# The last stage of a hybrid attention block on whole rows of 1024 columns, with the embedding vectors loaded earlier and the scalings behind the next tile's statistics

## The chip, the cores and the metric

The kernel runs on one core of a Trainium2 chip. Five kinds of engine work beside each other on it: TensorE (PE, its weight loads PEld) multiplies matrices into PSUM, VectorE (DVE) and ScalarE (ACT) work elementwise, GpSimd (POOL) does small work and issues the accumulating transfers, SyncE (SP) issues most of the others. The metric is the device time of one execution in microseconds; lower is better.

## The reference, cut to what matters

A block of a decoder: 16 meta tokens are put ahead of 512 rows of x, a layer norm with the embedding vectors `emb_ln_g` and `emb_ln_b` gives h, two attention branches run on one input projection, and their gated outputs are merged. The last stage adds the merged product to h, scaled by `DN_ALPHA`, normalizes each row of 1024 and applies `ln_g` and `ln_b`.

```python
h = layer_norm(concatenate([meta, x]), emb_ln_g, emb_ln_b)
for i in range(DEPTH):                              # DEPTH = 1
    proj = einsum('bld,dn->bln', h, w_in[i])        # ten parts of 1024 columns
    ...                                             # differential and stick-breaking attention: y_d, y_s
    br_d = einsum('blw,wd->bld', y_d * silu(g_d), w_br_diff[i])
    br_s = einsum('blw,wd->bld', y_s * silu(g_s), w_br_sb[i])
    merged = sigmoid(m_d + b_gate[i, 0]) * br_d + sigmoid(m_s + b_gate[i, 1]) * br_s
    y = einsum('bld,de->ble', merged, w_out[i])
    h = layer_norm(DN_ALPHA * h + y, ln_g[i], ln_b[i])
return h[:, N_META:]
```

## The kernel before, in words

All products are done in a fast fp32 form on split operands: a value a is a rounded high half and the remainder (a − high), and a product is three matmuls, high × high, high × low, low × high. The weights come as blocks of 128 × 512 (256 KB) through rings of buffers (`fetch`, line 144), ScalarE casts the high half (`hi`, line 183: `wh`), VectorE subtracts for the remainder (`lo`, line 188: `wl`). `wh` and `wl` are two tags with six buffers each; a block is split four blocks ahead of its use (`prep`).

The program has three parts. The start (norm of h, first queries) and everything behind the attention are fixed in the order in which they are written (`keep_order`). Between them lie 16 attention units (8 differential, 8 stick-breaking, interleaved with the projections of the next units); there a planner, which keeps its own timeline of engines and waits, sets the order on each engine. The later 11 units get keys and values by a seven-product scheme (line 690), and the two branch outputs too (`pair`, line 1065: pairs "BD" and then "BS", four each, with p from 0 to 3).

The last stage multiplies the merged rows (`MH`, `ML`) with the output weight in halves of 512 columns, `wo0` and `wo1`, each with its high and low half (`split_out`, lines 1126 and 1127, eight blocks of k per half). The loop runs over the two column halves c and, inside, over four row tiles t of 128 rows. A tile and half are 24 matmuls (line 1190) into one of three PSUM buffers; the last tile of the second half is done in two pieces of 256 columns. VectorE then adds the product to the scaled residual (line 1198) and takes statistics (line 1201). The residual, h again from x, is two VectorE instructions (lines 1161 and 1162) on 512 columns, done in the list `MEANWHILE` behind the tile's matmuls. Rows of x (`hr`) and the vectors (`eg`, `eb`) are loaded in halves of 512 by `load_half` into buffers of `wh` and `wl`; all eight `hr` halves and four vector halves are in place of twelve split weights.

When a tile has its second half, the statistics are aggregated (line 1206), GpSimd makes the reciprocal deviation `rs` in two small instructions (lines 296 and 297), and VectorE does, per 512 columns, a shift (line 1211: subtract the mean, times `ln_g`) and a scaling (line 1215: times `rs`, plus `ln_b`), in the order shift, scaling, shift, scaling, before it turns to the next tile. In the last tile ScalarE and GpSimd do the scaling of the last 256 columns (lines 1221 and 1222). SyncE writes the halves out (line 1227). `ln_g` and `ln_b` (`lgb`) are loaded by ScalarE's queue in the first tile, into buffers of the tag "two".

## Time and profile before

| | |
|---|---|
| time, median of 3 runs | 712.08 us (711.63 to 712.46) |
| profiled execution | 712.22 us, its span 710.4 us |
| busy: TensorE, VectorE, ScalarE, GpSimd | 697.5, 571.8, 439.2, 125.6 us |
| mean granted TensorE clock | 0.995 |
| last stage on TensorE | from 656.4 to 700.7 us |

The times on the right of a profile row are microseconds; in a timeline the first number is the start from the beginning of the span, the second the duration, and in brackets stands how long the engine was idle before and for what it waited. Matmuls overlap, so a busy TensorE is not yet one at its peak.

### The profile page before, as it was taken

To read this page: it belongs to the slowest core of one execution; us is meant where nothing else is said; L and a number is where in the kernel's file an instruction comes from. 1 tells how busy PE (TensorE), PEld (TensorE's weight loads), DVE (VectorE), ACT (ScalarE), POOL (GpSimd) and SP (SyncE) were. 2 spreads that over 40 slices of the span, in tenths; PEclk is the share of its full clock that TensorE was granted. 3 is DMA by queue.
4 is the path that set the end of the run, shared out by engine and by line. 5 is a ranking of instruction groups with operands and counts; after the bars stand their busy time and mean duration, and the time that the engine had idled before them with its cause. 6 is when DMAs were issued, how large, how long until landed. Compare 5 with 4: busy or idle time off the path is not lost.

```text
span 710.4 us, 13389 instructions
## 1 busy us (share of the span) xinstructions
PE 697.5 (98%) x4494; PEld 636.9 (90%) x4494; DVE 571.8 (80%) x1265; ACT 439.2 (62%) x1065; POOL 125.6 (18%) x143
## 2 busy tenths in 40 slices
PE   9999999999999999999999999999999999999994
PEld 8999999989999898988989998988889998999884
DVE  6888897878787777988878889976666788788897
ACT  5766676757667587776857777666455546455300
POOL 3214210212222111212123120000012102220002
PEclk9999999999999999999999999999999999999997
DMA  9368754879888876899897976646576748795902
GB/s 293 93 169 164 167 133 125 184 181 183 198 200 184 201 177 164 186 215 214 200 217 174 206 171 175 166 133 197 178 174 112 164 123 182 133 198 170 322 15 104
DMA packets 182182, 123.36 MB, mean 174 GB/s; under 512 B 9009, under 2 KB 165074, under 8 KB 182114
## 3 DMA queue, kind: packets, MB, share of 16 engines
q1 hardware_dynamic: 148130, 102.32, 50.1%
q0 software_dynamic: 33664, 19.14, 21.6%
q10 hardware_dynamic: 320, 1.06, 0.4%
q8 instruction: 35, 0.57, 0.3%
q14 instruction: 33, 0.27, 0.1%
HBM read 91.96 MB, written 9.44 MB: 143 GB/s over the span
## 4 chain that ended last, share of the span: by engine, by line
PE 86%; DVE 6%; DMA 3%; ACT 2%; issue 1%; POOL 1%; SPq 0%; ACTq 0%; DVEq 0%; POOLq 0%
PE q L690 16%; PE ps L496 12%; PE ps L494 12%; PE ps L495 12%; PE q L1065 10%; PE ps L510 7%; PE sc L754 6%; PE t L766 4%; DMA lgb<-in_ln_b_dram 1%; PE bank L385 1%; PE tv L723 1%; DVE hr L1215 1%; DMA xt<-in_x_dram 1%; PE av L922 1%; DMA raw<-in_w_out_dram 1%
## 5 line engine op out<-in xcount | busy, mean ns | idle before, releaser
L188 DVE TENSOR_TENSOR wl<-raw,wh 128x512 fp32r<-128x512 f32 x169 | 115.7, 691 | 43.7 <-ACT wh L183 42.2
L494 PE MATMUL ps<-hTh,wh 128*128 128x512 f32 x368 | 145.0, 394 | 0.0
L495 PE MATMUL ps<-hTl,wh 128*128 128x512 f32 x368 | 144.5, 393 | 0.0
L496 PE MATMUL ps<-hTh,wl 128*128 128x512 f32 x368 | 144.4, 392 | 0.0
L183 ACT CAST wh<-raw 128x512 fp32r<-128x512 f32 x169 | 104.4, 625 | 28.0 <-PE ps L495 15.3
L496 PEld LDWEIGHTS ps<-hTh,wl 128*128 128x128 f32 x368 | 69.2, 188 | 13.9
L495 PEld LDWEIGHTS ps<-hTl,wh 128*128 128x128 f32 x368 | 69.2, 188 | 13.1
L494 PEld LDWEIGHTS ps<-hTh,wh 128*128 128x128 f32 x368 | 69.2, 188 | 12.9
L146 POOL DMA_DIRECT2D rawk<-in_w_in_dram x44 | 60.8, 1642 | 96.9 <-DMA rawk<-in_w_in_dram 58.4
L754 PE MATMUL sc<-k,A 128*128 128x264 f32 (+3 forms) x320 | 65.9, 299 | 0.1
L1065 PE MATMUL q<-gh,wh 128*128 128x256 f32 x224 | 63.5, 283 | 0.2 <-ACT t L1074 0.2
L1065 PE MATMUL q<-gl,wh 128*128 128x256 f32 x224 | 63.4, 283 | 0.0
L1065 PE MATMUL q<-gh,wl 128*128 128x256 f32 x224 | 63.4, 283 | 0.0
L907 DVE TENSOR_TENSOR_SCAN e<-e,diag 128x528 f32<-128x528 f32 (+1 forms) x64 | 53.4, 848 | 7.5 <-ACT e L901 7.3
L754 PEld LDWEIGHTS sc<-k,A 128*128 128x128 f32 x320 | 50.3, 189 | 3.3 <-ACT e L901 0.3
L690 PE MATMUL q<-tS,wh 128*128 128x264 f32 x176 | 50.9, 290 | 0.9 <-DVE low L612 0.9
L690 PE MATMUL q<-tl,wh 128*128 128x264 f32 x176 | 50.2, 286 | 0.0
L690 PE MATMUL q<-tS,wl 128*128 128x264 f32 x176 | 50.2, 286 | 0.0
L510 PE MATMUL ps<-hTh,wh 128*128 128x264 f32 x160 | 46.4, 290 | 0.2 <-ACT k L632 0.2
L933 POOL DMA_DIRECT2D ys<-half x14 | 11.8, 840 | 195.9 <-ACT ys L932 119.2
L510 PE MATMUL ps<-hTh,wl 128*128 128x264 f32 x160 | 45.6, 286 | 0.0
L510 PE MATMUL ps<-hTl,wh 128*128 128x264 f32 x160 | 45.5, 285 | 0.0
(291 smaller groups left out, 1851.4 us busy)
## 6 DMA issues: line engine op xcount, KB each, us to landing
raw<-in_w_in_dram SPq DMA_DIRECT2D x141, 256.0 KB, 3.3
rawk<-in_w_in_dram POOLq DMA_DIRECT2D x44, 256.0 KB, 6.0
rawk<-in_w_in_dram SPq DMA_DIRECT2D x33, 256.0 KB, 3.9
k<-ks SPq DMA_DIRECT2D x60, 132.0 KB, 3.1
raw<-in_w_out_dram SPq DMA_DIRECT2D x16, 256.0 KB, 3.9
k<-ks SPq DMA_DIRECT2D x60, 66.0 KB, 2.8
A<-low SPq DMA_DIRECT2D x28, 128.0 KB, 2.8
raw<-in_w_br_diff_dram SPq DMA_DIRECT2D x12, 256.0 KB, 4.7
```

The costliest lines, as they stand in the source:

```text
L146: second[l] = [lambda raw=raw, x=x: g.dma_start(raw, x, accum_op=ALU.add) for x in more]
L183: s.copy(wh, raw)
L188: eng.tensor_tensor(wl, raw, wh.bitcast(F32), op=ALU.subtract)
L494: pe.matmul(ps, wh[:, k % 4, :], hTh[:, k, M:], start=(k == 0), stop=False)
L495: pe.matmul(ps, wh[:, k % 4, :], hTl[:, k, M:], start=False, stop=False)
L496: pe.matmul(ps, wl[:, k % 4, :], hTh[:, k, M:], start=False, stop=(k == KT - 1))
L510: pe.matmul(ps[:, :H2], a[:, k % 4, :], b[:, k, ts(c, H2)], start=(k == 0 and m == 0), stop=(k == KT - 1 and m == 2))
L690: pe.matmul(bank, a[:, k, :], b, start=start and k == 0 and j == 0, stop=k == 3 and j == 2, skip_group_check=not start)
L754: pe.matmul(ps[:, :n], q, K[:, m, k0:k0 + n], start=(m == 0), stop=(m == 1))
L766: pe.transpose(t[:, o:o + P], a[:, AOFF[i] + j * P:AOFF[i] + (j + 1) * P], ident)
L907: v.tensor_tensor_scan(rev, rev, diag[0][:, L - nk:][:, ::-1], 0.0, ALU.mult, ALU.max)
L1065: pe.matmul(bank, a[:, k, :], b[:, n, k, :], start=start and k == 0 and m == 0, stop=k == 3 and m == 2, skip_group_check=not start)
```

## The change

The split weights' halves share one tag `w2`: a buffer holds the high and the low half of a block. The rows of x, `hr`, become one buffer of 1024 columns per row tile, in the place of one split block, and so do `ln_g` and `ln_b`. The embedding vectors are whole too; they take buffers of the tag "two" and are loaded ahead of the second pair of the second branch (p = 1). The residual, the shift and the scaling are one instruction on 1024 columns each (the last tile scales in two halves). The scaling of a tile is held in `unfinished` until the next tile has its statistics; the third tile's follows its own shift at once. ScalarE and GpSimd have no part in the last tile's columns any more. The output is written by whole rows, the last tile by halves. `ln_g` and `ln_b` are loaded in the third tile of the first column half.

```diff
@@ -178,7 +178,8 @@
         item = items[h]
         assert not second.get(item)
         raw = raw0[:, h // 2, ts(h % 2, 4)] if item is None else sums.pop(h) if isinstance(item, tuple) else raws[item]
-        wh, wl = [wpool.tile([P, 4, P], F32R, tag=w, name=w, bufs=6) for w in ("wh", "wl")]
+        w2 = wpool.tile([P, 2, 4, P], F32R, tag="w2", name="w2", bufs=6)
+        wh, wl = w2[:, 0], w2[:, 1]
         split.append((raw, wh, wl))
         s.copy(wh, raw)
 
@@ -1133,8 +1134,13 @@
         state["ahead"] += 1
         prep(len(split))
 
+    vec = {}
     for p in range(4):
         steps = []
+        if p == 1:
+            for name, src in (("eg", emb_g), ("eb", emb_b)):
+                vec[name] = pair_of(name, n=512).rearrange("p a b -> p (a b)")
+                nc.sync.dma_start(vec[name], src.partition_broadcast(P))
         if p == 3:
             run([merge_gate(1, 7, MS[7])], [(4.4, further)])
             WO = [[hpool.tile([P, KT, 512], F32R, tag=f"hT{x}", name=f"wo0{x}") for x in "hl"]]
@@ -1142,46 +1148,39 @@
         run([pair("BS", p, G, MS[2 * p:2 * p + 2], lambda m, p=p: merged(2 * p + m))], steps)
 
 
-    def half(tag, name):
-        return wpool.tile([P, 4, P], F32, tag=tag, name=name, bufs=6).rearrange("p a b -> p (a b)")
-
-    vec, hrs = {}, [[None, None] for t in range(NB)]
-
-    def load_half(c):
-        tag = ("wh", "wl")[c]
-        for name, src in (("eg", emb_g), ("eb", emb_b)):
-            vec[name, c] = half({"eg": "wh", "eb": "wl"}[name], name)
-            nc.sync.dma_start(vec[name, c], src[ts(c, 512)].partition_broadcast(P))
-        for t in range(NB):
-            hrs[t][c] = half(tag, "hr")
-            nc.sync.dma_start(hrs[t][c], x[0, ts(t, P), ts(c, 512)])
-
-    def residual(t, c):
-        hr = hrs[t][c]
-        v.scalar_tensor_tensor(hr, hr, xmv[:, t, 0:1], vec["eg", c], op0=ALU.subtract, op1=ALU.mult)
-        v.scalar_tensor_tensor(hr, hr, xrs[:, t:t + 1], vec["eb", c], op0=ALU.mult, op1=ALU.add)
+    def whole(name):
+        return wpool.tile([P, 2, 4, P], F32, tag="w2", name=name, bufs=6).rearrange("p a b c -> p (a b c)")
+
+    hrs = []
+
+    def load_rows(t):
+        hrs.append(whole("hr"))
+        nc.sync.dma_start(hrs[t], x[0, ts(t, P), :])
+
+    def residual(t):
+        hr = hrs[t]
+        v.scalar_tensor_tensor(hr, hr, xmv[:, t, 0:1], vec["eg"], op0=ALU.subtract, op1=ALU.mult)
+        v.scalar_tensor_tensor(hr, hr, xrs[:, t:t + 1], vec["eb"], op0=ALU.mult, op1=ALU.add)
 
     for _, f in later:
         f()
     later.clear()
-    load_half(0)
     for k in range(5, KT):
         split_out(0, k)
-    load_half(1)
+        if k == 5:
+            load_rows(0)
     WO.append([lp.tile([P, KT, 512], F32R, tag=f"g{x}", name=f"wo1{x}") for x in "hl"])
-    lgb = [pair_of("lgb", n=512) for j in range(2)]
-    lgb = [t.rearrange("p a b -> p (a b)") for t in lgb]
+    lgb, unfinished = [], []
     sts = [lr.tile([P, 4, 6], F32, tag="fst", name="fst", bufs=4) for t in range(NB)]
-    MEANWHILE = [[lambda: residual(0, 0)] + [lambda k=k: split_out(1, k) for k in range(3)],
-                 [lambda: residual(1, 0)] + [lambda k=k: split_out(1, k) for k in range(3, 6)],
-                 [lambda: residual(2, 0)] + [lambda k=k: split_out(1, k) for k in range(6, 8)] + [lambda: residual(0, 1)],
-                 [lambda: residual(3, 0)] + [lambda t=t: residual(t, 1) for t in range(1, 3)],
-                 [lambda: residual(3, 1)], [], [], []]
+    MEANWHILE = [[lambda k=k: split_out(1, k) for k in range(3)] + [lambda: residual(0), lambda: load_rows(1)],
+                 [lambda k=k: split_out(1, k) for k in range(3, 6)] + [lambda: residual(1), lambda: load_rows(2)],
+                 [lambda k=k: split_out(1, k) for k in range(6, 8)] + [lambda: residual(2), lambda: load_rows(3)],
+                 [lambda: residual(3)], [], [], [], []]
     for c in range(2):
         for t in range(NB):
             st, final = sts[t], t == NB - 1
             for o, w in [(0, 256), (256, 256)] if final and c else [(0, 512)]:
-                r, hr = ds(o, w), hrs[t][c]
+                r, hr = ds(o, w), hrs[t][:, ts(c, 512)]
                 ps = pj.tile([P, 512], F32, tag="pj", name="pso")[:, :w]
                 products = [(k, m) for k in (0, 1, 2, 3, 4, 5, 7, 6) for m in ("hh", "hl", "lh")]
                 if t == 0 and c == 0:
@@ -1192,9 +1191,10 @@
                 if o == 0:
                     for work in MEANWHILE[NB * c + t]:
                         work()
-                    if t == 0 and c == 0:
-                        nc.scalar.dma_start(lgb[0][:, :], ln_g[0].partition_broadcast(P))
-                        nc.scalar.dma_start(lgb[1][:, :], ln_b[0].partition_broadcast(P))
+                    if t == 2 and c == 0:
+                        for src in (ln_g, ln_b):
+                            lgb.append(whole("lgb"))
+                            nc.scalar.dma_start(lgb[-1], src[0].partition_broadcast(P))
                 v.scalar_tensor_tensor(hr[:, r], hr[:, r], DN_ALPHA, ps, op0=ALU.mult, op1=ALU.add)
                 w = 256 if final else 512
                 for n in range(o // w, 2 if final and not c else o // w + 1):
@@ -1206,25 +1206,30 @@
             v.bn_aggr(mv, st[:, :4 if final else 2])
             rstd_of(lr, mv[:, 1:2], rs, P)
 
-            def shift(c, o, w):
-                a = hrs[t][c][:, ds(o, w)]
-                v.scalar_tensor_tensor(a, a, mv[:, 0:1], lgb[0][:, ds(512 * c + o, w)], op0=ALU.subtract, op1=ALU.mult)
-
-            def scale(c, o, w):
-                a = hrs[t][c][:, ds(o, w)]
-                v.scalar_tensor_tensor(a, a, rs, lgb[1][:, ds(512 * c + o, w)], op0=ALU.mult, op1=ALU.add)
-
-            shift(0, 0, 512)
-            if final:
-                a = hrs[t][1][:, 256:]
-                shift(1, 256, 256)
-                s.mul(a, a, rs)
-                g.tensor_tensor(a, a, lgb[1][:, 768:], op=ALU.add)
-            scale(0, 0, 512)
-            shift(1, 0, 256 if final else 512)
-            scale(1, 0, 256 if final else 512)
-            for h in range(2):
-                nc.sync.dma_start(out[0, ts(t, P), ts(h, 512)], hrs[t][h])
+            def shift(o, w, t=t, mv=mv):
+                a = hrs[t][:, ds(o, w)]
+                v.scalar_tensor_tensor(a, a, mv[:, 0:1], lgb[0][:, ds(o, w)], op0=ALU.subtract, op1=ALU.mult)
+
+            def scale(o, w, t=t, rs=rs):
+                a = hrs[t][:, ds(o, w)]
+                v.scalar_tensor_tensor(a, a, rs, lgb[1][:, ds(o, w)], op0=ALU.mult, op1=ALU.add)
+
+            def finish(scale=scale, t=t):
+                scale(0, D)
+                nc.sync.dma_start(out[0, ts(t, P), :], hrs[t])
+
+            if unfinished:
+                unfinished.pop()()
+            shift(0, D)
+            if not final:
+                unfinished.append(finish)
+                if t == NB - 2:
+                    unfinished.pop()()
+                continue
+            scale(0, 512)
+            nc.sync.dma_start(out[0, ts(t, P), :512], hrs[t][:, :512])
+            scale(512, 512)
+            nc.sync.dma_start(out[0, ts(t, P), 512:], hrs[t][:, 512:])
     keep_order(state["ends"], ORDERED[:1])
     keep_order(first, ORDERED + [mybir.EngineType.SP])
 
```

Three places show what this does to the order. First SyncE's queue, from the end of the second branch to the end of the program. Before (`raw` of `in_w_out` are blocks of the output weight):

```order
L144 DMA raw<-in_w_out_dram 128x512 x11
L1154 DMA eg<-in_emb_ln_g_dram 128x512
L1154 DMA eb<-in_emb_ln_b_dram 128x512
L1157 DMA hr<-in_x_dram 128x512 x4
L144 DMA raw<-in_w_out_dram 128x512 x3
L1154 DMA eg<-in_emb_ln_g_dram 128x512
L1154 DMA eb<-in_emb_ln_b_dram 128x512
L1157 DMA hr<-in_x_dram 128x512 x4
L144 DMA raw<-in_w_out_dram 128x512 x2
L1227 DMA out_dram<-hr 128x512 x8
```

With the change (`raw` and `rawa` of `in_w_br_sb` are the last pair's weights, lines are counted in the new file):

```order
L1143 DMA eg<-in_emb_ln_g_dram 128x1024
L1143 DMA eb<-in_emb_ln_b_dram 128x1024
L144 DMA raw<-in_w_in_dram 128x4x128
L144 DMA raw<-in_w_br_sb_dram 128x4x128
L144 DMA rawa<-in_w_br_sb_dram 128x4x128 x2
L144 DMA raw<-in_w_br_sb_dram 128x4x128 x2
L144 DMA raw<-in_w_out_dram 128x512 x12
L1158 DMA hr<-in_x_dram 128x1024
L144 DMA raw<-in_w_out_dram 128x512 x4
L1158 DMA hr<-in_x_dram 128x1024 x3
L1219 DMA out_dram<-hr 128x1024 x3
```

The vectors moved ahead of the last pair's weights; one row load stands between the twelfth and thirteenth block of the output weight, the other three behind the last block.

Second VectorE in the last column half, the third tile and the beginning of the last. Before (`pso` is the product, `fst` the statistics, `fmv` mean and variance, `frs` the reciprocal deviation):

```order
L1198 SCALAR_TENSOR_TENSOR hr<-hr,pso 128x512
L1201 BN_STATS fst<-hr 128x6
L1206 BN_AGGR fmv<-fst 128x2
L1211 SCALAR_TENSOR_TENSOR hr<-hr,fmv,lgb 128x512
L1215 SCALAR_TENSOR_TENSOR hr<-hr,frs,lgb 128x512
L1211 SCALAR_TENSOR_TENSOR hr<-hr,fmv,lgb 128x512
L1215 SCALAR_TENSOR_TENSOR hr<-hr,frs,lgb 128x512
L1198 SCALAR_TENSOR_TENSOR hr<-hr,pso 128x256
```

With the change:

```order
L1198 SCALAR_TENSOR_TENSOR hr<-hr,pso 128x512
L1201 BN_STATS fst<-hr 128x6
L1206 BN_AGGR fmv<-fst 128x2
L1215 SCALAR_TENSOR_TENSOR hr<-hr,frs,lgb 128x1024
L1211 SCALAR_TENSOR_TENSOR hr<-hr,fmv,lgb 128x1024
L1215 SCALAR_TENSOR_TENSOR hr<-hr,frs,lgb 128x1024
L1198 SCALAR_TENSOR_TENSOR hr<-hr,pso 128x256
```

The first scaling is the second tile's, the other two wide instructions are the third tile's.

Third VectorE in the first attention unit, where the planner sets the order (`e` the exponentials, `apad` their normalized difference, `rz` the reciprocal sums, the ISA rows the bias and maximum of the next block). Before:

```order
L834 ISA e_447,mn<-sc,bias 128x272
L834 ISA mn 128x1
L843 TENSOR_SCALAR rz<-rz,nlam 128x1
L844 TENSOR_SCALAR e_446<-e_446,rz 128x400
L664 TENSOR_TENSOR hF<-hF 128x264
L845 SCALAR_TENSOR_TENSOR apad_433<-e_447,rz,e_446 128x400
```

With the change (buffer numbers differ, lines are one higher):

```order
L844 TENSOR_SCALAR rz<-rz,nlam 128x1
L845 TENSOR_SCALAR e_442<-e_442,rz 128x400
L835 ISA e_443,mn<-sc,bias 128x272
L835 ISA mn 128x1
L665 TENSOR_TENSOR hF<-hF 128x264
L846 SCALAR_TENSOR_TENSOR apad_429<-e_443,rz,e_442 128x400
```

The two small normalizing steps moved ahead of the bias of the next block. Rows change places like this in many positions of the 16 units on TensorE, VectorE, ScalarE and SyncE; no line of the source there is another than before but the buffers of the split weights.

## The prediction

> **What bounds the kernel now.** The page comes first: the span, TensorE's busy time, and then who TensorE waited for over the whole run.
>
> ```profile
> span 710.4 us, 13389 instructions
> PE 697.5 (98%) x4494; PEld 636.9 (90%) x4494; DVE 571.8 (80%) x1265; ACT 439.2 (62%) x1065; POOL 125.6 (18%) x143
> ```
>
> ```profile
> PE warm L306 <- POOL ident masks.py:199: 1.4, 1, 1.4
> PE q L690 <- DVE low L612: 0.9, 2, 0.6
> PE bank L339 <- DVE xn L335: 0.3, 1, 0.3
> PE ps L510 <- ACT k L632: 0.2, 1, 0.2
> PE q L1065 <- ACT t L1074: 0.2, 1, 0.2
> ```
>
> TensorE is the bound until the last stage: all its listed waits come to 3.0 us, and only 0.9 + 0.2 + 0.2 = 1.3 us of them lie behind the start. So a better order of the middle can bring hardly more than 1.3 us. What is left is the end; here is the last full window of 10 us.
>
> ```profile
> 700.00:710.00 10.00, 0.68 (x6) 0.47 (x4) 7.06 (x13) 0.51 (x1) 1.78 (x3) 0.64 0.27 106
> ```
>
> The columns are TensorE, its weight loads, VectorE, ScalarE, GpSimd, granted clock, DMA. TensorE stops just behind 700, and VectorE works on. The timeline of both around the last two row tiles says how far behind it is (start, duration).
>
> ```profile
> 678.45 0.39 PE L1190 MATMUL pso<-wo1h,mh 128*128 128x512 f32 x1
> 694.54 0.39 PE L1190 MATMUL pso<-wo1h,ml 128*128 128x512 f32 x1
> 697.52 0.28 PE L1190 MATMUL pso<-wo1h,ml 128*128 128x256 f32 x1
> 700.40 0.28 PE L1190 MATMUL pso<-wo1h,ml 128*128 128x256 f32 x1
> ```
>
> ```profile
> 683.78 0.68 DVE L1198 SCALAR_TENSOR_TENSOR hr<-hr,pso 128x512 f32<-128x512 f32 x1
> 686.61 0.68 DVE L1198 SCALAR_TENSOR_TENSOR hr<-hr,pso 128x512 f32<-128x512 f32 x1
> 696.93 0.68 DVE L1198 SCALAR_TENSOR_TENSOR hr<-hr,pso 128x512 f32<-128x512 f32 x1
> 697.64 0.69 DVE L1201 BATCH_NORM_STATS2 fst<-hr 128x6 f32<-128x512 f32 x1
> 698.37 0.21 DVE L1206 BATCH_NORM_AGGREGATE fmv<-fst 128x2 f32<-128x12 f32 x1
> 698.62 0.78 DVE L1211 SCALAR_TENSOR_TENSOR hr<-hr,fmv,lgb 128x512 f32<-128x512 f32 x1
> 699.84 0.75 DVE L1215 SCALAR_TENSOR_TENSOR hr<-hr,frs,lgb 128x512 f32<-128x512 f32 x1 [0.44 <-POOL frs L297]
> 700.50 0.74 DVE L1211 SCALAR_TENSOR_TENSOR hr<-hr,fmv,lgb 128x512 f32<-128x512 f32 x1
> 701.95 0.41 DVE L1198 SCALAR_TENSOR_TENSOR hr<-hr,pso 128x256 f32<-128x256 f32 x1
> 703.64 0.26 DVE L1206 BATCH_NORM_AGGREGATE fmv<-fst 128x2 f32<-128x24 f32 x1
> 705.16 0.75 DVE L1215 SCALAR_TENSOR_TENSOR hr<-hr,frs,lgb 128x512 f32<-128x512 f32 x1
> 705.83 0.97 DVE L1211 SCALAR_TENSOR_TENSOR hr<-hr,fmv,lgb 128x256 f32<-128x256 f32 x1
> 706.83 0.48 DVE L1215 SCALAR_TENSOR_TENSOR hr<-hr,frs,lgb 128x256 f32<-128x256 f32 x1
> ```
>
> The third row tile's product is complete at 694.54 + 0.39 = 694.93, and VectorE takes it at 696.93: 2.0 us late. The last tile's two halves are complete at 697.80 and 700.68, and VectorE turns to the first at 701.95. VectorE, not TensorE, sets the end; its last instruction ends at 707.31, and 710.4 − 707.31 = 3.1 us of output transfer and closing follow. The lag was inherited: the last tile of the first column half is summed at 683.78, a residual follows, and the second half begins at 686.61, while TensorE does the three whole tiles of that half from 678.45 to 694.93, 5.5 us each: the first was complete at about 683.9.
>
> **The change part by part.** *Wide instructions.* What does 1024 columns cost on VectorE? The trace has this form at 256 and 512, and one two-operand operation at 1024.
>
> ```profile
> L1162 DVE SCALAR_TENSOR_TENSOR hr<-hr,xrs,eb 128x512 f32<-128x512 f32 x8 | 6.0, 752 | 0.3
> L1215 DVE SCALAR_TENSOR_TENSOR hr<-hr,frs,lgb 128x256 f32<-128x256 f32 x1 | 0.5, 485 | 0.0
> L1047 DVE TENSOR_TENSOR gl<-t,gh 128x1024 fp32r<-128x1024 f32 x4 | 4.9, 1226 | 0.7 <-ACT gh L1046 0.7
> ```
>
> From 256 to 512 is 0.267 us, so 512 more make 0.752 + 0.534 = 1.29 us. Bounds: 1.23 (the wide row above) and 2 × 0.75 = 1.50 (no saving). I take 1.29, as it is the same operation. An instruction that does not need the one ahead of it starts some 0.08 us before that one ends (699.84 to 700.50 is 0.66 for 0.75), so the step is then 1.21. A residual (two of them, the second needs the first) goes from 2 × (0.75 + 0.66) = 2.82 to 1.29 + 1.21 = 2.50 us per row tile.
> [...]
>
> *Loads.* By the order rows of SyncE in the section on the change, two embedding vectors (512 KB each) go ahead of the last branch pair's weights; the last two blocks of the output weight no longer stand behind rows of x. What that does to VectorE:
>
> ```profile
> 659.43 1.89 DVE L1127 TENSOR_TENSOR wo0l<-raw,wo0h 128x512 fp32r<-128x512 f32 x3
> 663.03 0.75 DVE L1161 SCALAR_TENSOR_TENSOR hr<-hr,xmv,eg 128x512 f32<-128x512 f32 x1 [1.71 <-DMA hr<-in_x_dram]
> 675.43 1.33 DVE L1127 TENSOR_TENSOR wo1l<-raw,wo1h 128x512 fp32r<-128x512 f32 x2 [1.06 <-ACT wo1h L1126]
> ```
>
> ```profile
> raw<-in_w_in_dram SPq DMA_DIRECT2D x141, 256.0 KB, 3.3
> raw<-in_w_in_dram SPq DMA_DIRECT2D x4, 512.0 KB, 6.1
> hr<-in_x_dram SPq DMA_DIRECT2D x8, 256.0 KB, 5.9
> lgb<-in_ln_b_dram ACTq DMA_DIRECT2D x1, 512.0 KB, 10.3
> ```
>
> With the change VectorE does three remainders up to 661.3, three of the second half's (1.9) up to 663.2, then needs the first rows. They are issued right behind the twelfth weight block, whose buffer the first of those remainders frees, so at about 660.5; 512 KB take 6.1 us (bounds: 3.3, of the quicker 256 KB loads, and 10.3), so 666.6. VectorE waits 3.4 us in place of 1.71, but the 1.06 at 675.43 goes. From 666.6: residual 2.5, sum and statistics 1.4, remainders 1.9, then 2.5 + 1.4 + 1.25, 2.5 + 1.4, 2.5 + 1.45: the first column half is finished at 685.4 (before: the sum of 683.78, then statistics and one more residual, up to 686.61).
>
> *The last column half.* By the order rows of VectorE there, the second tile's scaling fills the time in which GpSimd works on the third tile's deviation, so the 0.44 wait goes; but the third tile pays two scalings. Work of VectorE: first tile 0.71 + 0.73 + 0.25 + 1.3 = 3.0, second 4.2, third 5.45; 12.65 in all. The third tile cannot start before 695.0, so this half may start as late as 695.0 − 7.2 = 687.8 without harm. It starts at 685.4: 2.4 us of cover for everything ahead.
> Third tile: sum 695.0, statistics 695.7, aggregate 696.45, scaling of the second tile 696.7, shift 697.9, its own scaling 699.2 (deviation ready 1.47 behind the aggregate, as from 698.37 to 699.84, so at 697.9), first half of the last tile 700.45 (before 701.95). Then as before: aggregate 703.64 − 701.95 = 1.69 later, 702.14. Shift of 1024 from 702.44 to 703.73; the deviation is there 1.52 behind the aggregate (703.64 to 705.16), at 703.66; two scalings of 512 end at 703.76 + 0.67 + 0.75 = 705.2. Before, 707.31: **2.1 us earlier**. ScalarE's and GpSimd's part on the last quarter, and the 0.97 of the shift beside GpSimd, are gone.
>
> *Output.* Fewer, larger writes; the last is still 256 KB, and its predecessor is issued 0.7 us ahead of it instead of 1.4.
>
> ```profile
> 690.56 17.15 SPq L1227 DMA_DIRECT2D out_dram<-hr  x8
> DMA to landing us min/median/max: 2.0/2.0/2.2
> ```
>
> I keep 3.1 us behind the last instruction, with 0 to 0.3 more for the closer spacing.
>
> *One buffer for both weight halves.* High and low half of a split weight now share a buffer, so ScalarE's cast waits for the last of the old block's three products instead of the second: 0.23 us of TensorE time, with four blocks of lead. That is hidden. But this wait enters the planner's view, and the middle of the program comes out in another order. In the order rows of the first attention unit, the normalizing now stands ahead of the next block's bias, and the like goes on through both attention kinds. Cost of it: from −1.3 us (every wait of TensorE gone) to, say, one more wait of 0.9 / 2 = 0.45 us in each of the 11 units that use line 690, +5.0. I take 0, since TensorE hardly waits and the work is the same.
>
> **Sum.** The profiled execution took 712.22 us in all for its span of 710.4, 0.14 above the median of 712.08. 712.22 − 2.1 = 710.1; from the median 710.0.
>
> **The rivals.**
> *A, rows of x late.* At 10.3 us the first rows land at 670.8, 4.2 us later than assumed; the cover is 2.4, so 1.8 of the 2.1 is lost: 711.8. Against it: the 10.3 was measured among 2 MB of rows and vectors, which now come earlier or later.
> *B, the planner's new order costs TensorE time (the slower side).* All 11 waits of 0.45 give 710.0 + 5.0 = 715.0; it is a loss from 2.1 us, five such waits, and measurably one from 3.5, eight of them. For it: the old order had two such waits, the rows moved are very many. Against it: both orders are made by the same rules. A part of it, 0.7 to 3.5 us, ends within 0.2% of before.
> *C, the embedding vectors hold up the second branch.* They are put in at about 618, before a stretch in which the DMA engines are full:
>
> ```profile
> 620.00:630.00 10.00, 10.00 (x85) 10.00 (x84) 8.07 (x16) 5.71 (x12) 2.35 (x3) 1.00 0.99 220
> 617.00 1.28 POOL L146 DMA_DIRECT2D rawa<-in_w_br_sb_dram  x1 [4.21 <-DVE t L1076]
> 625.59 0.62 ACT L183 CAST wh<-rawa 128x512 fp32r<-128x512 f32 x1
> ```
>
> 1.05 MB at 220 GB/s are 4.8 us. The block whose second part GpSimd adds by a transfer issued at 617.00 is cast at 625.59; with the 5.9 us that a row of x takes (a loaded queue) it was there at 622.9, 2.7 us early. TensorE takes it four products of twelve later, 4 × 12 × 10 / 85 = 5.6 us. Together 8.3 us of cover for 4.8. Without that cover: 714.8.
> [...]
> *D, the new order is better:* 710.0 − 1.3 = 708.7.
>
> **Chances.** The forecast 0.62, A 0.08, B whole 0.08 and in part 0.12, C 0.03, D 0.07. The own range of the forecast: 1.50 for a wide instruction costs 4 × 0.21 = 0.8, and the output 0.3 more, 711.1; 1.23 gives 709.7. Range for 8 in 10: 708.7 (D) to 712.5 (B with 2.5 us). A difference of 0.2% is 1.4 us, about what a measurement here can tell. Faster, below 710.65: most of the forecast and D, 0.65; same: A, B in part, the forecast's poor end, 0.24; slower 0.11.
>
> **What would show it.** Wide instructions of lines 1211 and 1162 at 1.29 us; VectorE idle ahead of the second and third tile's sums in the last column half; the last tile's first sum about 700.5 relative to TensorE's end at 700.7; the last VectorE instruction 4.5 us behind TensorE's last product instead of 6.6. Waits of TensorE behind the start near 1.3 us. It is wrong if TensorE's last product comes more than 1 us later than at 700.4, if its waits list line 690 or 1065 with several us, or if a wide instruction takes 1.5.

## The result, and the profile after

| | before | after |
|---|---|---|
| time, median (lowest to highest) of 22 runs each | 712.12 us (711.38 to 714.36) | 713.63 us (711.72 to 715.44) |
| profiled execution, its span | 712.22 us, 710.4 us | 714.06 us, 712.3 us |
| TensorE's last product ends | 700.68 us | 703.99 us |
| VectorE's last instruction ends | 707.31 us | 709.08 us |
| from TensorE's end to VectorE's | 6.6 us | 5.1 us |

The ratio is 1.0017 (95% interval 1.0010 to 1.0025): the change makes the kernel about 0.2% slower. The forecast was 710.0 us and faster, so it is wrong in sign and outside its range. The last rows of the table split the difference of the two profiled executions: TensorE finishes 3.3 us later, the tail behind it is 1.5 us shorter, and 3.2 us of output and closing follow instead of 3.1; 3.3 − 1.5 + 0.1 = 1.9, the difference of the spans.

The head of the page of the changed kernel:

```profile
span 712.3 us, 13321 instructions
PE 697.1 (98%) x4494; PEld 636.1 (89%) x4494; DVE 568.4 (80%) x1249; ACT 438.3 (62%) x1064; POOL 128.9 (18%) x142
```

TensorE's work is the same (697.1 us for 697.5) and VectorE has 3.4 us less to do, as the change intends. The 3.3 us must then be waits, and the list of what TensorE waited for names them (us in total, times, longest):

```profile
PE q L1066 <- ACT t L1071: 2.3, 1, 2.3
...
PE q L1066 <- ACT t L1075: 0.7, 1, 0.7
```

Line 1066 is a product of the second branch, line 1065 of the kernel before, where its waits came to 0.2 us. They lie ahead of the last stage: ScalarE copies out a product late, and TensorE has no PSUM buffer for the next.

In the last stage itself, the timeline of TensorE and VectorE on the changed kernel (start, duration):

```profile
703.71 0.28 PE L1189 MATMUL pso<-wo1h,ml 128*128 128x256 f32 x1
```

```profile
692.83 0.69 DVE L1198 SCALAR_TENSOR_TENSOR hr<-hr,pso 128x512 f32<-128x512 f32 x1 [2.41 <-PE pso L1189]
...
698.27 0.69 DVE L1198 SCALAR_TENSOR_TENSOR hr<-hr,pso 128x512 f32<-128x512 f32 x1 [1.42 <-PE pso L1189]
...
699.85 1.23 DVE L1215 SCALAR_TENSOR_TENSOR hr<-hr,frs,lgb 128x1024 f32<-128x1024 f32 x1
701.00 1.28 DVE L1211 SCALAR_TENSOR_TENSOR hr<-hr,fmv,lgb 128x1024 f32<-128x1024 f32 x1
702.72 1.29 DVE L1215 SCALAR_TENSOR_TENSOR hr<-hr,frs,lgb 128x1024 f32<-128x1024 f32 x1 [0.44 <-POOL frs L298]
703.92 0.41 DVE L1198 SCALAR_TENSOR_TENSOR hr<-hr,pso 128x256 f32<-128x256 f32 x1
...
705.61 0.26 DVE L1206 BATCH_NORM_AGGREGATE fmv<-fst 128x2 f32<-128x24 f32 x1
705.91 1.31 DVE L1211 SCALAR_TENSOR_TENSOR hr<-hr,fmv,lgb 128x1024 f32<-128x1024 f32 x1
707.66 1.42 DVE L1215 SCALAR_TENSOR_TENSOR hr<-hr,frs,lgb 128x512 f32<-128x512 f32 x2 [0.44 <-POOL frs L298]
```

VectorE now waits for TensorE ahead of the second and the third tile's sum (2.41 and 1.42 us): its lag is gone. But two waits of 0.44 us for GpSimd's deviation stand there, ahead of the third tile's scaling and of the last one. GpSimd's rows say why; the kernel before first, then the changed one:

```profile
698.66 0.19 POOL L296 TENSOR_TENSOR lne<-fmv,epsr 128x1 f32<-128x1 f32 x1 [3.89 <-DVE fmv L1206]
698.93 0.87 POOL L297 TENSOR_TENSOR frs<-lne,neghalf 128x1 f32<-128x1 f32 x1
```

```profile
700.01 1.12 POOL L297 TENSOR_TENSOR lne<-fmv,epsr 128x1 f32<-128x1 f32 x1 [2.75 <-DVE fmv L1206]
701.21 1.48 POOL L298 TENSOR_TENSOR frs<-lne,neghalf 128x1 f32<-128x1 f32 x1
705.96 0.19 POOL L297 TENSOR_TENSOR lne<-fmv,epsr 128x1 f32<-128x1 f32 x1 [3.27 <-DVE fmv L1206]
706.23 1.40 POOL L298 TENSOR_TENSOR frs<-lne,neghalf 128x1 f32<-128x1 f32 x1
```

The same two one-column instructions take 1.12 and 1.48 us instead of 0.19 and 0.87. Read beside VectorE: the first ends at 701.13, just behind VectorE's scaling (699.85 + 1.23 = 701.08); the second ends at 702.69, 0.41 behind VectorE's shift (701.00 + 1.28 = 702.28). In the kernel before, the second ended at 699.80, 0.40 behind the shift that ran beside it (698.62 + 0.78 = 699.40).

### The profile page after: what moved, and what is told of

Read it like the earlier page. It is cut to its first block, busy times and chain, and to the rows that moved or that the text cites. A ratio compares the mean times of both kernels' runs of the same rounds, so it can differ in the third digit from the quotient of the medians.

```text
span 712.3 us, 13321 instructions
## 1 busy us (share of the span) xinstructions
PE 697.1 (98%) x4494; PEld 636.1 (89%) x4494; DVE 568.4 (80%) x1249; ACT 438.3 (62%) x1064; POOL 128.9 (18%) x142
## 4 chain that ended last, share of the span: by engine, by line
PE 87%; ACT 3%; DMA 3%; issue 3%; DVE 2%; POOL 1%; POOLq 0%; DVEq 0%; SPq 0%; ACTq 0%
PE q L691 15%; PE ps L496 11%; PE ps L497 11%; PE ps L495 11%; PE q L1066 9%; PE ps L511 7%; PE pso L1189 5%; PE sc L755 5%; PE t L767 3%; DMA ss<-td 1%; PE bank L386 1%; PE tv L724 1%; DMA k<-ks 1%; PE av L923 1%; PE av L924 1%
## 5 line engine op out<-in xcount | busy, mean ns | idle before, releaser
L189 DVE TENSOR_TENSOR w<-raw,w 128x512 fp32r<-128x512 f32 x169 | 114.7, 685 | 44.1 <-ACT w L184 41.7
L495 PE MATMUL ps<-hTh,w 128*128 128x512 f32 x368 | 145.0, 394 | 0.0
L497 PE MATMUL ps<-hTh,w 128*128 128x512 f32 x368 | 144.6, 393 | 0.0
L496 PE MATMUL ps<-hTl,w 128*128 128x512 f32 x368 | 144.3, 392 | 0.0
L184 ACT CAST w<-raw 128x512 fp32r<-128x512 f32 x169 | 104.1, 626 | 19.0 <-PE ps L497 7.8
L1066 PE MATMUL q<-gh,w 128*128 128x256 f32 x448 | 81.6, 283 | 3.1 <-ACT t L1071 2.3
L497 PEld LDWEIGHTS ps<-hTh,w 128*128 128x128 f32 x368 | 69.2, 188 | 13.8
L496 PEld LDWEIGHTS ps<-hTl,w 128*128 128x128 f32 x368 | 69.2, 188 | 13.0
L495 PEld LDWEIGHTS ps<-hTh,w 128*128 128x128 f32 x368 | 69.2, 188 | 12.8
L691 PE MATMUL q<-tS,w 128*128 128x264 f32 x352 | 75.1, 290 | 0.0
L1066 PEld LDWEIGHTS q<-gh,w 128*128 128x128 f32 x448 | 70.2, 192 | 3.6 <-ACT t L1071 2.5
L511 PE MATMUL ps<-hTh,w 128*128 128x264 f32 x320 | 64.4, 288 | 0.2 <-ACT k L633 0.2
L511 PEld LDWEIGHTS ps<-hTh,w 128*128 128x128 f32 x320 | 51.4, 188 | 0.6 <-ACT k L633 0.4
```

Of the source, the lines that this page charges most:

```text
L184: s.copy(wh, raw)
L189: eng.tensor_tensor(wl, raw, wh.bitcast(F32), op=ALU.subtract)
L495: pe.matmul(ps, wh[:, k % 4, :], hTh[:, k, M:], start=(k == 0), stop=False)
L496: pe.matmul(ps, wh[:, k % 4, :], hTl[:, k, M:], start=False, stop=False)
L497: pe.matmul(ps, wl[:, k % 4, :], hTh[:, k, M:], start=False, stop=(k == KT - 1))
L511: pe.matmul(ps[:, :H2], a[:, k % 4, :], b[:, k, ts(c, H2)], start=(k == 0 and m == 0), stop=(k == KT - 1 and m == 2))
```

## Where TensorE lost its 3.3 us: the two traces side by side

The DMA issues (count, KB each, median us from issue to landing), before and after:

```profile
sm<-sm POOLq DMA_DIRECT2D x2, 256.0 KB, 3.9
...
ss<-sm POOLq DMA_DIRECT2D x1, 256.0 KB, 6.6
```

```profile
eg<-in_emb_ln_g_dram SPq DMA_DIRECT2D x1, 512.0 KB, 7.1
eb<-in_emb_ln_b_dram SPq DMA_DIRECT2D x1, 512.0 KB, 7.6
sm<-sm POOLq DMA_DIRECT2D x2, 256.0 KB, 7.9
ss<-sm POOLq DMA_DIRECT2D x1, 256.0 KB, 10.4
```

`sm<-sm` and `ss<-...` are the accumulating transfers with which GpSimd's queue merges the two branches (`merged`, line 1112). The vectors are issued at 618.54 and 619.42, the two transfers on `sm` from 620.75: they take 4.0 us longer than before. What follows on GpSimd's queue, before and after (the weight adds, which add the second part of a weight block to the first, and then the merging transfers on `ss`):

```profile
629.40 2.62 POOL L146 DMA_DIRECT2D rawa<-in_w_br_sb_dram  x2 [7.04 <-ACT mh L1106]
631.24 1.69 POOL L1115 DMA_DIRECT2D ss<-td  x1
```

```profile
632.57 2.62 POOL L146 DMA_DIRECT2D rawa<-in_w_br_sb_dram  x2 [10.02 <-ACT t L1071]
634.25 1.85 POOL L1116 DMA_DIRECT2D ss<-td  x1
```

And ScalarE, which rounds the merged rows (`mh`) at places in its order that are fixed when the program is written (`rounded`, put into `later` six steps behind the transfer), before and after:

```profile
621.92 0.37 ACT L1070 COPY t<-q 128x256 f32<-128x256 f32 x1 [2.27 <-PE q L1065]
...
626.11 0.62 ACT L1106 CAST mh<-sm 128x512 fp32r<-128x512 f32 x1
...
637.93 0.62 ACT L1106 CAST mh<-ss 128x512 fp32r<-128x512 f32 x1 [1.62 <-DMA ss<-td]
...
639.41 0.62 ACT L1106 CAST mh<-ss 128x512 fp32r<-128x512 f32 x1 [0.34 <-DMA ss<-sm]
...
647.72 0.37 ACT L1070 COPY t<-q 128x256 f32<-128x256 f32 x1
```

```profile
622.11 0.37 ACT L1071 COPY t<-q 128x256 f32<-128x256 f32 x1 [2.21 <-PE q L1066]
...
628.34 0.62 ACT L1107 CAST mh<-sm 128x512 fp32r<-128x512 f32 x1 [1.94 <-DMA sm<-sm]
...
643.29 0.62 ACT L1107 CAST mh<-ss 128x512 fp32r<-128x512 f32 x1 [6.33 <-DMA ss<-td]
...
645.25 0.62 ACT L1107 CAST mh<-ss 128x512 fp32r<-128x512 f32 x1 [0.82 <-DMA ss<-sm]
...
651.04 0.37 ACT L1071 COPY t<-q 128x256 f32<-128x256 f32 x1
```

The late `sm` transfers do not carry the delay further. ScalarE's cast waits 1.94 us for them where it waited for nothing, but its first copy of the third pair comes 10.08 us behind that of the second in both kernels (632.00 − 621.92 and 632.19 − 622.11). What makes the weight adds late is the load of their own blocks by SyncE, before and after, and the time of these two loads to landing in the changed kernel:

```profile
624.64 1.11 SPq L144 DMA_DIRECT2D rawa<-in_w_br_sb_dram  x2
```

```profile
625.25 1.88 SPq L144 DMA_DIRECT2D rawa<-in_w_br_sb_dram  x2
```

```profile
rawa<-in_w_br_sb_dram SPq DMA_DIRECT2D x2, 256.0 KB, 6.7
```

The semaphore records of the traces have the first of these loads landing at 628.81 before and at 631.98 after, 4.2 and 6.7 us behind its issue. The weight add starts 0.59 us behind that landing in both (629.40 and 632.57). The ScalarE instructions named in the brackets of the GpSimd rows keep no such distance: their ends lie 0.2 us ahead of the add in one row and at its very start in the other.

The chain: the loads of the next weight blocks, issued 6 to 7 us behind the vectors, land late; GpSimd's weight adds go out at 632.57 instead of 629.40. The `ss` transfer behind them on the queue goes out at 634.25 instead of 631.24, although the VectorE step that it needs (line 1084) had ended at 631.6, and takes 9.0 us instead of 6.7. ScalarE stands still 6.33 us instead of 1.62, and everything behind that cast on ScalarE moves with it: the weight casts, and at the end the copy of line 1071 for which TensorE waits. In the chain of what ended last that transfer has a row of its own:

```profile
634.25 9.02 DMA ss<-td
```

The vectors have landed by 627.1 (619.42 + 7.6), ahead of the `ss` transfer. What lengthens it then is not shown; other traffic that the vectors pushed back is an argument, not a measurement.

For the experiments this gives two measures that do not depend on where a run starts. The first copies of the second and of the last weight pair (621.92 and 647.72) are 25.80 us apart before and 28.93 after; the 3.13 more is the stall. And from the last pair's copy to TensorE's last product it is 52.68 us before (700.40 − 647.72) and 52.67 after (703.71 − 651.04), so nothing else delays TensorE.

## The experiments

Theories: **1**, the early vectors make the merging transfers late, and TensorE pays for it as above. **2**, the planner's new order of the middle costs TensorE time (the prediction's rival B). **G**, GpSimd's deviation is held beside the wide VectorE instructions and takes part of the tail's gain. The comparison kernel in each case is the kernel before, run on the same chip in the same batch (medians 712.08 to 712.21 us).

**The vectors behind the second branch** (the change, with this alone undone)

```diff
-        if p == 1:
-            for name, src in (("eg", emb_g), ("eb", emb_b)):
-                ...                                  # load, whole
...
     later.clear()
+    for name, src in (("eg", emb_g), ("eb", emb_b)):
+        ...                                          # load, whole
```

> The changed kernel with one edit: the two embedding vectors are loaded behind the second branch (where the kernel before loaded its first halves) instead of ahead of its second pair. Theory 1 (the early vectors hold up GpSimd's adding transfers of the merged rows; ScalarE waits in order for them, and TensorE then waits on ScalarE's copies, 2.3 and 0.7 us on line 1066): these two waits fall to about 0.2 us, TensorE's last product comes back from 703.7 to about 700.5, the time falls by 3 us to about 710.6. Theory 2 (the planner's new order of the middle costs the time): waits and time stay, 713.6 within 0.4. Under theory 1 VectorE may wait a little longer for the first rows, since 1 MB now stands ahead of them.

Measured: 711.04 us (11 runs), ratio 0.9985 (0.9976 to 0.9994). The copies are 25.80 apart, TensorE's waits on line 1066 are back at 0.2 us, and `sm<-sm` lands in 3.8 us. VectorE's last instruction ends 5.1 us behind TensorE's, with the same two waits of 0.44. So the early vectors cost 713.63 − 711.04 = 2.6 us, and the rest of the change gains 1.2 us.

**Shared buffers alone** (the kernel before, with the split weights' halves in one buffer; rows and vectors loaded in halves as before)

```diff
-        wh, wl = [wpool.tile([P, 4, P], F32R, tag=w, name=w, bufs=6) for w in ("wh", "wl")]
+        w2 = wpool.tile([P, 2, 4, P], F32R, tag="w2", name="w2", bufs=6)
+        wh, wl = w2[:, 0], w2[:, 1]
```

> The kernel before with one edit: the halves of a split weight share a buffer (and the halves of x rows and vectors are put into such buffers); loads, last stage and all else as before. TensorE's order is then that of the changed kernel. Theory 1 (the new order is harmless): 712.1 within 0.4, TensorE reaches line 1065 within 0.3 us of 542.7. Theory 2 (the new order costs): 713.3 or more, with waits of TensorE between 100 and 540 us.

Measured: 712.12 us (11 runs), ratio 1.0002 (0.9993 to 1.0010). Up to the second branch TensorE, VectorE and ScalarE do their work in the changed kernel's order. The copies are 25.81 apart. Theory 2 falls: the new order costs nothing that can be measured.

**The vectors alone** (the kernel before, with the old order and the old last stage; only the vectors loaded whole ahead of the second pair, and `ln_g`, `ln_b` in the buffers of their former halves)

```diff
+        if p == 1:
+            for name, src in (("eg", emb_g), ("eb", emb_b)):
+                vec[name] = pair_of(name, n=512).rearrange("p a b -> p (a b)")
+                nc.sync.dma_start(vec[name], src.partition_broadcast(P))
```

> The kernel before with one edit: the two embedding vectors are loaded whole ahead of the second pair of the second branch, in the buffers that ln_g and ln_b had, and these go in halves into the buffers that become free; the middle keeps the old order. Theory 1: TensorE waits 2 to 3 us on line 1065, and the time rises to 714 to 715, less up to 1 us that VectorE gains at the end because fewer loads stand ahead of the output weight. Theory 2: no wait, 712.1 within 0.4 or slightly less.

Measured: 713.35 us (12 runs), ratio 1.0019 (1.0008 to 1.0030). The copies are 29.69 apart. The lists of waits of TensorE and of ScalarE in this kernel:

```profile
PE q L1065 <- ACT t L1070: 2.8, 1, 2.8
```

```profile
ACT mh L1106 <- DMA ss<-td: 6.6, 1, 6.6
```

Moving this load alone into the old kernel brings both the loss and its place. The profiled execution (715.55 us) is 2.2 us longer than the median, so the stall in it, 3.9 us, is above the usual; part of it comes back at the end, where VectorE's last instruction ends 4.7 us behind TensorE's last product instead of 6.6. With the first run, theory 1 holds in both directions: taken out of the change the loss goes, put into the kernel before it comes.

**VectorE merges two of the rows** (the change; of the six merging transfers the two in the middle become VectorE additions: those on `ss` for which ScalarE waited 6.33 and 0.82 us)

```diff
-        wait = 6 if j < 6 else 1
-        if j < 6:
+        by_dma = j in (0, 1, 4, 5)
+        wait = 6 if by_dma else 1
+        if by_dma:
```

> The changed kernel with one edit: the second pair's two merged rows (j = 2 and 3) are added by VectorE instead of by GpSimd's adding transfers; the vectors stay where they are. Theory 1 in its whole chain (the adding transfers into ss are what ScalarE waits for): ScalarE's 6.3 us wait for ss<-td goes, TensorE's two waits fall to about 0.2 us, and the time falls by about 3 us to 710.6 or, with VectorE's two added sums of 0.7 us, to 711. If instead the vectors hold up the weights themselves, ScalarE waits for those and TensorE's waits stay at about 3 us and the time at 713.6.

Measured: 713.25 us (12 runs, up to 717.78), ratio 1.0021 (1.0009 to 1.0034). Not a cure; the time is that of the second case of the expectation, in which the vectors hold up the weights themselves. The profiled execution is the longest of the twelve, so its sizes are not typical, but its waits show where the loss went: the transfers on `sm` take 9.2 us to landing, ScalarE's casts of them wait 3.8 us in all, and TensorE waits 3.3 us on line 1066. GpSimd's weight adds are late here too, and their row names the load:

```profile
634.37 2.62 POOL L146 DMA_DIRECT2D rawa<-in_w_br_sb_dram  x2 [11.24 <-DMA rawa<-in_w_br_sb_dram]
```

The run does not test the `ss` transfers alone. With `wait` at 1 instead of 6 the two casts also move forward in ScalarE's order, ahead of the third pair's first copy; they wait there 1.24 and 1.13 us for VectorE's sums, and that copy comes 14.4 us behind the second pair's instead of 10.1. How much of the loss this move made is not shown. The `ss` transfers as the one weak link are not confirmed by it.

**The vectors one pair earlier** (p = 0 instead of p = 1, issued at 607.79)

> The changed kernel with the vectors loaded one pair earlier, ahead of the first pair of the second branch. Theory 1 in the form that is left (the vectors delay whatever transfers share the DMA engines with them, and it costs time where ScalarE is due to wait for such a transfer in order): issued at about 607, they run into a stretch in which the DMA engines are busy 0.70 (605 to 610) and then 0.20 (610 to 615). So the waits on line 1066 are at most 0.5 us and the time 710.6 to 711.6. If any load of 1 MB in this branch costs 3 us, 713.3 or more.

Measured: 711.04 us (11 runs), ratio 0.9985 (0.9976 to 0.9994). The transfers on `sm` take 4.9 us, the copies are 25.80 apart. The same megabyte inside the same branch, 11 us earlier, costs nothing: it has landed (608.34 + 8.2 = 616.5) before the merging begins at 620.7 and before the two weight loads go out at 625.4, which land within 4.0 us.

**One of the two vectors early** (`eg` at p = 1, `eb` behind the branch)

> The change with half of the load inside the second branch: the first embedding vector (512 KB) stays ahead of the branch's second weight pair, the second is loaded behind the branch. Theory 1 (the early vectors make the adding transfers late, and TensorE waits for what the last of them releases): the adding transfer on sm is lengthened by half as much, to about 5.9 us from issue to landing (3.9 before, 7.9 with both vectors), ScalarE's cast behind it and the transfers on ss run some 2 us late instead of 4.4; with about 1 us of slack in that chain TensorE stalls about 1 us on line 1066: about 712.2 us. If it is not the volume but the place alone that counts (any transfer put ahead of that weight pair), 713.5 as with both. If the chain has more slack than 2 us, 711.0 as with none.

The page's line, and ScalarE's second `ss` cast and its last first copy:

```profile
sm<-sm POOLq DMA_DIRECT2D x2, 256.0 KB, 5.0
```

```profile
640.29 0.62 ACT L1107 CAST mh<-ss 128x512 fp32r<-128x512 f32 x1 [0.39 <-DMA ss<-sm]
...
648.05 0.37 ACT L1071 COPY t<-q 128x256 f32<-128x256 f32 x1
```

Measured: 710.98 us (10 runs), ratio 0.9984 (0.9974 to 0.9994); no stall. The expectation of theory 1, 712.2, was too high: half the volume lengthens the transfer by 1.1 us, not by 2.0, the weight adds go out 0.1 us later and the cast of `ss` comes 0.6 us later (both counted from the first copy), which the slack takes up.

**Both vectors one pair later** (p = 2, issued at 628.94 and 629.49)

> The change with both vectors loaded one weight pair later in the second branch (ahead of its third pair, issued some 12 us later than in the change, when the adding transfer on sm has landed, close to the transfers on ss). Theory 1 in its narrow form (the transfer on sm at 620 us is the sensitive one, since everything that follows on GpSimd's queue is issued behind it): that transfer takes 3.9 us again, the ones on ss some 4 us longer, and TensorE loses less than in the change, 711 to 712.5. Theory 1 in its wide form (each adding transfer is as sensitive): ScalarE's cast behind the ss transfer comes as late, TensorE stalls 2 to 4 us on line 1066, 713 to 714.5. If the time between the vectors and the end of the branch matters for the second pair's weights alone, 711.0.

```profile
sm<-sm POOLq DMA_DIRECT2D x2, 256.0 KB, 3.9
...
ss<-sm POOLq DMA_DIRECT2D x1, 256.0 KB, 10.3
```

```profile
643.66 0.62 ACT L1107 CAST mh<-ss 128x512 fp32r<-128x512 f32 x1 [0.41 <-DMA ss<-sm]
...
649.87 0.37 ACT L1071 COPY t<-q 128x256 f32<-128x256 f32 x1
```

Measured: 712.73 us (10 runs), ratio 1.0007 (0.9997 to 1.0017): between the two forms of the theory, just above the narrow one. The transfer on `sm` is as before, the one on `ss` is hit in its place, and TensorE stalls 1.64 us. The narrow form had the `sm` transfer as the sensitive one, and a stall without it speaks against that. At p = 1 the loss is larger because there the weight adds ahead of the `ss` transfers are late as well: they go out 10.46 us behind the first copy at p = 1 (632.57 − 622.11), 7.40 at p = 2 (629.83 − 622.43) and 7.48 before.

Together, in us from the first copy (second pair) to the cast of `ss` behind the second transfer and to the last pair's copy:

| kernel | first copy at | to the second cast of `ss` | to the last pair's copy | stall |
|---|---|---|---|---|
| before | 621.92 | 17.49 | 25.80 | 0 |
| vectors behind the branch | 623.24 | 17.32 | 25.80 | 0 |
| one vector early | 622.25 | 18.04 | 25.80 | 0 |
| vectors at p = 0 | 622.09 | 18.96 | 25.80 | 0 |
| vectors at p = 2 | 622.43 | 21.23 | 27.44 | 1.64 |
| the change | 622.11 | 23.14 | 28.93 | 3.13 |
| vectors alone, old kernel | 622.00 | 23.90 | 29.69 | 3.89 |

In the last three rows the stall stands 19.6 to 20.0 us short of the cast (21.23 − 1.64, 23.14 − 3.13, 23.90 − 3.89): up to there the cast may be late without harm. Before, it stood at 17.49. The cover was 20.0 − 17.5 = about 2.5 us, and the vectors made the cast 23.14 − 17.49 = 5.65 us late. The row of the vectors alone is from an execution longer than usual, as said above.

**Shift and scaling in pieces of 512** (the vectors behind the branch, and each wide instruction of the last column half made two)

```diff
             def shift(o, w, t=t, mv=mv):
+                if w == D:
+                    shift(0, 512, t, mv)
+                    return shift(512, 512, t, mv)
             ...
             def scale(o, w, t=t, rs=rs):
+                if w == D:
+                    scale(0, 512, t, rs)
+                    return scale(512, 512, t, rs)
```

> The kernel with the vectors behind the branch (711.04 us) with one edit: shift and scaling of the last column half are done in two instructions of 512 columns each instead of one of 1024. Theory G (GpSimd's two small instructions for the deviation stand still while a VectorE instruction runs, so a wide one holds them longer): from aggregate to deviation about 1.5 to 1.9 us instead of 2.97 in the third tile, GpSimd's instructions at most 0.9 us, VectorE's two waits of 0.44 us go; VectorE pays about 0.13 us more per pair of halves, so the time is 711.0 within 0.5. Rival (GpSimd is slow there for another reason): 2.97 stays, and the time is 0.4 to 0.6 us longer, 711.5.

GpSimd in the third tile of this kernel:

```profile
697.35 0.58 POOL L297 TENSOR_TENSOR lne<-fmv,epsr 128x1 f32<-128x1 f32 x1 [3.83 <-DVE fmv L1205]
698.02 0.94 POOL L298 TENSOR_TENSOR frs<-lne,neghalf 128x1 f32<-128x1 f32 x1
```

Measured: 710.53 us (11 runs), ratio 0.9981 (0.9971 to 0.9991). Beside instructions of half the length GpSimd takes 0.58 and 0.94 us instead of 1.12 and 1.48; both waits of 0.44 go, and VectorE ends 4.54 us behind TensorE instead of 5.10, although the pairs of narrow instructions cost it some 0.1 us each (1.36 to 1.44 for two, 1.23 to 1.31 for one).

**The deviation on ScalarE** (the vectors behind the branch; wide instructions kept)

```diff
+                        s.preload_act_table_set("natural_log_exp_and_others")
...
-            rstd_of(lr, mv[:, 1:2], rs, P)
+            s.activation(rs, mv[:, 1:2], AF.Ln, bias=epsr)
+            s.activation(rs, rs, AF.Exp, scale=-0.5)
```

> The kernel with the vectors behind the branch with one edit: ScalarE makes the reciprocal deviation of the last stage (logarithm, exponential) instead of GpSimd; its table is loaded behind its last cast. Theory G: the deviation is there about 1 us behind the aggregate, VectorE's two waits of 0.44 us go, and the last VectorE instruction ends about 4.3 us behind TensorE's last product instead of 5.1; 710.2 us. Rival: the waits go, but as much is lost elsewhere (ScalarE's instructions of one column are slow too), 711.0.

ScalarE and VectorE in the third tile of this kernel:

```profile
696.74 0.29 ACT L1207 ACTIVATE frs<-fmv,epsr 128x1 f32<-128x1 f32 x1 [4.91 <-DVE fmv L1206]
697.07 0.20 ACT L1208 ACTIVATE frs<-frs 128x1 f32<-128x1 f32 x1
```

```profile
699.16 1.28 DVE L1216 SCALAR_TENSOR_TENSOR hr<-hr,frs,lgb 128x1024 f32<-128x1024 f32 x1
```

Measured: 710.19 us (11 runs), ratio 0.9972 (0.9964 to 0.9981). The deviation is there 0.8 us behind the start of the aggregate (696.50 to 697.27) instead of 3.0, VectorE waits for nothing, and its end lies 4.40 us behind TensorE's. ScalarE is not held beside the same wide VectorE instructions: its second instruction ends at 697.27, while VectorE's scaling runs from 696.62 to 697.85. Theory G holds for the third tile: beside a longer VectorE instruction GpSimd's pair takes longer (0.58 and 0.94 us beside 512 columns, 1.12 and 1.48 beside 1024), while ScalarE's takes 0.29 and 0.20 beside 1024. This kernel has the lowest median of all, 2.0 us below the kernel before; the 0.3 us to the one with pieces of 512 lie within the scatter of the runs.

**The same, with the vectors inside the first branch** (issued at 570.89)

> As the kernel before it (deviation on ScalarE), and the vectors are loaded ahead of the last pair of the first branch, issued at about 569 us, where the DMA engines are busy 0.2 to 0.4. Theory 1: no wait of TensorE comes from it, and the first rows of x arrive earlier than with the vectors behind the branch; 709.5 to 710.2. If early vectors cost time wherever they stand, 712 or more.

Measured: 710.38 us (11 runs), ratio 0.9975 (0.9966 to 0.9983), the tail at 4.41 us, the copies 25.80 apart. No different from the kernel ahead: once the vectors are out of the merging's way, loading them still earlier brings nothing.

## Why the prediction was wrong, by its own steps

- **The failed step is rival C, in the sentence "Together 8.3 us of cover for 4.8".** It followed one weight block from its transfer to TensorE, and gave the whole case 0.03. That block was on time: its cast comes 3.67 us behind the first copy in both kernels (625.59 − 621.92 and 625.78 − 622.11). The delay went another way. The loads of the next two blocks of its kind, issued 6 to 7 us behind the vectors, took 6.7 us instead of 4.2; the weight adds that wait for them stand on GpSimd's queue ahead of the merging transfers on `ss`; and ScalarE awaits those in a fixed place of its order. The cover on that way was about 2.5 us, and the cast came 5.65 us late. The trace of before showed how tight it was: the `ss` cast already waited 1.62 us for its transfer. The prediction asked for whom TensorE waits, and did not ask who waits, in order, for each transfer that shares the window. That the load of the vectors makes the loss is shown by runs in both directions; the way from it to TensorE is read from the traces.
- The size in C was fair: 4.8 us of volume, against the 5.65 us of the cast and 3.1 of stall in the profile (2.6 between the medians). But the stretch that it called full, at a share of 0.99, took more, as the last section shows.
- **The deviation was mis-sized:** "1.47 behind the aggregate" measured 3.0 (699.72 to 702.69), and "1.52" for the last tile measured 2.0 (705.61 to 707.63). VectorE ended 5.1 us behind TensorE instead of 4.5. Where the hold is taken away it ends 4.5 or 4.4 behind, so the rest of that sum was right.
- Right: the wide instruction (1.23 to 1.31 us for 1.29); VectorE idle ahead of the second and third tile's sums, by 2.41 + 1.42 = 3.8 us, more than the 2.4 of cover, since the last column half began 16.5 us ahead of TensorE's end (703.99 − 687.46) where 15.3 was worked out (700.7 − 685.4); no cost for the shared buffers and the planner's new order; 3.2 us behind the last instruction for 3.1. With both errors mended the sum's −2.1 us came out as 712.15 − 710.19 = −2.0.
- Rival A (late rows of x) did not come: VectorE waits 1.80 us for the first rows in the change and 1.95 with the vectors behind the branch, less than the 3.4 allowed for.
- Of the conditions that were to show it wrong, two came true as written: TensorE's last product more than 1 us later than 700.4, and several us on line 1065, now 1066.

## What to carry to other kernels

Before a load is moved, list every transfer in flight in its new window, on all queues, what is issued behind it on an ordered queue, and for each the engine that waits for it in a fixed order, with how long that wait has been idle: the smallest of these covers counts, not the bound engine's own. A named releaser is worth a second look: where its distance to the instruction differs from trace to trace, another that keeps its distance (0.59 us in both traces here) is the likelier one. A wait that already shows, like the 1.62 us of the `ss` cast in the kernel before, can be a place without much cover (2.5 us here), even where the bound engine does not feel it yet. And where small GpSimd instructions stand on a path, look at VectorE's instructions beside them before these are made longer: here, in the third tile, the two took 1.12 and 1.48 us beside 1024 columns and 0.58 and 0.94 beside 512; a short ScalarE pair in their place (0.29 and 0.20 us) was not held.

## What the runs showed of the hardware that was not expected

In the third tile of the change GpSimd's two one-column instructions end 0.05 and 0.41 us behind the VectorE instruction beside which they run (701.13 for 701.08, 702.69 for 702.28), after 1.12 and 1.48 us beside 1024 columns. In the kernel with pieces of 512 they take 0.58 and 0.94, and the second ends at 698.96, 0.41 behind VectorE's second piece of the scaling (the two run from 697.19 to 698.55). Not each one is held: of two that start 0.05 us behind VectorE's shift in the changed kernel, the one at 705.96 takes 0.19 us (shift at 705.91), the one at 689.19 takes 1.28 (shift from 689.14 to 690.42). The kernel before shows a hold the other way round: VectorE's shift of 256 columns at 705.83, which starts 0.04 us behind GpSimd's addition on the last columns (705.79 to 706.51), takes 0.97 us instead of the 0.47 of the one ahead of it. The runs show these holds and their length, not their cause. With the 0.40 us by which the second instruction ended behind the shift in the kernel before, the deviation in the third tile comes out of the prediction's own numbers: held to the end of the shift that it put at 697.9, so ready at 697.9 + 1.29 + 0.40 = 699.6, 3.1 us behind the aggregate of 696.45 instead of 1.47; 3.0 was measured.

A DMA share of 0.99 in the window from 620 to 630 us was not a ceiling. With the vectors in it, the same window reads:

```profile
620.00:630.00 10.00, 10.00 (x86) 10.00 (x85) 7.66 (x15) 4.51 (x10) 1.75 (x2) 1.00 1.08 280
```

The engines moved 280 GB/s instead of 220, 0.6 MB more in 10 us, so more than half of the vectors' 1.05 MB was added to the other traffic rather than put in its place. So the prediction's reading of 0.99, DMA engines that are full, does not hold. The accumulating transfers beside them still took twice their time (7.9 us for 3.9), and the weight loads 6.7 us for 4.2. What makes the delay is not shown by these runs.
